# Four sequence mixers with their FFNs on one core: later head scaling, casts and roots on other engines, and another scheduling mode for the order

## The chip, the cores and the metric

The kernel runs on one core of a Trainium2 chip. TensorE (PE in the profile) multiplies matrices, VectorE (DVE), ScalarE (ACT) and GpSimd (POOL) work on tiles, and SyncE (SP) issues the transfers. Each engine works through its own instruction queue in order, and semaphores tie the queues together. The metric is the device time of one execution in microseconds: 1273.06 us for the kernel before (median of three runs, 1273.02 to 1274.07).

## The reference

Input is one sequence of 256 tokens with 1024 channels in float32. Four layers follow one another, with the mixers HGRN, mLSTM, S5 and HGRN again. After each mixer and after each FFN comes a residual with layer norm:

```python
x = _layernorm(ALPHA * x + h, ln_g[i, 0], ln_b[i, 0])
x = _layernorm(ALPHA * x + _swiglu(x, w_gate_up, w_down), ln_g[i, 1], ln_b[i, 1])
```

The HGRN mixer projects x to queries, forget gates, values and output gates, 8 heads of 128 channels. Its recurrence is computed in parallel form: scores of queries and keys with decay products, times the values. What comes out of a head is scaled by the root of its mean square, multiplied by the output gate, and projected:

```python
o = _head_rmsnorm(_from_chunks(oc), norm_w)          # o * rsqrt(mean(o*o) + eps) * w
o = o.reshape(bsz, seq, D_MODEL) * jax.nn.silu(g)
return o @ w_out
```

mLSTM is a matrix memory with exponential gates, S5 a complex diagonal scan of 64 groups with 64 states, and the FFN is SwiGLU with 2816 hidden channels.

## The kernel before

Every float32 operand of a large product is split in a high and a low part, and each product is three matmuls (`mm3`, L155 to L157; the wide form is L185 and L188). Weights come in units of 1 MB on SyncE's queue. Of each half unit ScalarE casts the high part (L127) and VectorE subtracts it to get the low part (L128); I call an L128 on weights a split. Activations lie transposed in `xx`, high and low, ready as matmul operands. A layer norm (`norm`, L205 to L240) takes token half h: residual and statistics (L221 to L223), the root of the variance (`rsqrt`: a multiply and add L197 and a power L198, both on GpSimd), subtract and scale (L235, L236), a transpose on TensorE (L240), and the split into `xx` (L259 on ScalarE, L260 on VectorE). The last norm has no transpose; it scales in two pieces per half (L228, L230) and each piece is sent to the output.

The HGRN mixer (`hgrn`) works on score groups of two head pairs, (0, 1) and (2, 3). For each, `hgrn_scores` first makes the scores within 32 tokens (L606, L607), then runs levels m = 1, 2, 4, 8, 16, 32, 64: ScalarE copies keys (L616), TensorE makes a small product (L620, and L629 for m = 32 and 64), VectorE puts it in place (L623) and multiplies queries and keys with the decay products of the next level (L592). L652 then makes the scores across the halves. Between the levels the program text puts pieces of the projections for values (`v1`) and output gates (`g0`, `g1`), 144 matmuls in all; they are independent of the scores. `heads_out(n)` makes the outputs of four heads (L505, L507), their squares (L509) and sums (L510), the root on GpSimd, and the scaling (L515); `turn` multiplies by the gate (L519) and transposes (L413).

The S5 mixer runs eight blocks: TensorE makes a block's inputs (L1115), VectorE turns them, scans them and turns them back (L1158 to L1169, state in `s5hs`), TensorE makes the outputs of two blocks (L1127) and transposes them (L1133), and L1138 writes the low part of the transposed outputs, for which the output projection waits.

The program text does not fix the order of instructions. `tile.TileContext` schedules the whole program when it is built: it chooses the order within each engine's queue from the dependencies, the program's order, priorities and its own estimate of when things are ready. What stands in a queue then stays in that order on the chip.

The last FFN block (`dproj` with `j == last and i == 3`, L338) orders its matmuls by output columns, then by token halves. At the start, `warm_up` issues matmuls on zeros (L74) and `begin` splits the first pieces of x and of the first weights with `halve`, as their transfers land.

Of the kernel before, what the change touches and what calls it, by code (L numbers as in the profile page):

```python
# [17 lines left out]
P = 128  # L18
# [16 lines left out]
class Trunk:  # L35
    def __init__(self, ctx, tc, aps):
        self.ctx, self.tc, self.nc, self.a = ctx, tc, tc.nc, aps
        mk = lambda name, bufs, **kw: ctx.enter_context(tc.tile_pool(name=name, bufs=bufs, **kw))
        self.const = mk("const", 1)
        self.stage = mk("stage", 3)  # L40
        self.split = mk("split", 8)
        self.xp = mk("xp", 3)
        self.gbp = mk("gbp", 1)
        self.small = mk("small", 4)
        self.ps = mk("ps", 2, space=bass.MemoryType.PSUM)
        self.dram = mk("dram", 1, space=bass.MemoryType.DRAM)
        self.n = 0
        c = self.const
        self.ident = c.tile([P, P], F32, name="ident")
        self.root = c.tile([P, 8], F32, name="root")  # L50
        self.nc.gpsimd.memset(self.root, -0.5)
        self.xx = c.tile([P, KD, 2, S], F32R, name="xx")
# [14 lines left out]
    def warm_up(self, pool):  # L67


        z = pool.tile([P, 512], BF16, name="warm")  # L70
        self.nc.vector.memset(z, 0.0)
        ps = self.bank("t")
        for _ in range(7):
            self.nc.tensor.matmul(ps, z[:, 0:P], z, start=True, stop=True)  # L74


# [53 lines left out]
    def begin(self, pool):  # L130

        src = pool.tile([P, KD, S + 512], F32, name="first")
        out = [self.pair() for _ in range(4)]
        for k, n in ((0, 1), (1, 1), (2, 1), (3, 1), (4, 2), (6, 2)):
            self.nc.sync.dma_start(src[:, k : k + n], self.a["first"][:, k : k + n])
            self.halve(src[:, k : k + n, 0:S], self.xh[:, k : k + n], self.xl[:, k : k + n])
            wide = lambda y: (y if n == 2 else y[:, k % 2 * 512 : (k % 2 + 1) * 512]).rearrange("p (k c) -> p k c", k=n)
            self.halve(src[:, k : k + n, S:], *(wide(y) for y in out[k // 2]))
        for i in range(2):
            self.ready[self.plan[i]] = out[2 * i : 2 * i + 2]  # L140
        self.staged = 2
        self.nc.sync.dma_start(self.ident, self.a["c_ident"])
# [50 lines left out]
    def rsqrt(self, v, n, eps, mul=1.0):  # L193

        t = self.small.tile([P, 2, 8], F32, tag="rs", name=self.uid("rs"))
        w, q = t[:, 0, :n], t[:, 1, :n]
        self.nc.gpsimd.tensor_scalar(w, v, mul, eps, ALU.mult, ALU.add)  # L197
        self.nc.gpsimd.tensor_tensor(q, w, self.root[:, 0:n], ALU.pow)  # L198
        return q

# [13 lines left out]
    def norm(self, h, banks, gb, last=None, perm=False, rev=False):  # L214
# [6 lines left out]
            nc.vector.scalar_tensor_tensor(z[:, c], self.x[h][:, c], ALPHA, banks[n], ALU.mult, ALU.add)  # L221
            nc.vector.bn_stats(st[:, n, :], z[:, c])
        nc.vector.bn_aggr(mv, st)  # L223
        r = self.rsqrt(mv[:, 1:2], 1, LN_EPS)
        if last is not None:
            cuts = slice(0, 512), slice(512, D)
            for c in cuts:
                nc.vector.scalar_tensor_tensor(z[:, c], z[:, c], mv[:, 0:1], gb[:, 0, c], ALU.subtract, ALU.mult)  # L228
            for c in cuts:
                nc.vector.scalar_tensor_tensor(z[:, c], z[:, c], r, gb[:, 1, c], ALU.mult, ALU.add)  # L230
                nc.sync.dma_start(last[h * P : (h + 1) * P, c], z[:, c])
            return
# [213 lines left out]
    def hgrn(self, j, gb, lb=None):  # L446
# [3 lines left out]
        with tc.tile_pool(name=self.uid("hg"), bufs=1, reuse_waits="tile") as hp, \  # L450
# [44 lines left out]
            def heads_out(n):  # L495
# [13 lines left out]
                    nc.scalar.activation(s, po[h], AF.Square)  # L509
                    nc.vector.tensor_reduce(ss[:, h], s.rearrange("p (a b) -> p a b", a=4), AX.X, ALU.add)  # L510
                r = self.rsqrt(ss.rearrange("p a b -> p (a b)"), 8, HEAD_EPS, 1.0 / P)
                for h in range(2):
                    on[n, h] = wp.tile([P, 512], F32, tag="q", name=self.uid("on"), bufs=4)
                    f4 = lambda x: x.rearrange("p (a b) -> p a b", a=4)
                    nc.vector.tensor_tensor(f4(on[n, h]), f4(po[h]), r[:, 4 * h : 4 * h + 4, None].broadcast_to([P, 4, P]), ALU.mult)  # L515

            def turn(n, h):
                o, gate = on[n, h], g[:, h, n * 512 : (n + 1) * 512]
# [35 lines left out]
            scores((2, 3), ([lambda: heads_out(0)], g0[0:1], g0[1:2], g0[2:3], g0[3:], g1[0:1], g1[1:2], g1[2:3]))  # L554
            gb = gb()
            g1[3]()
            for h in range(2):
                turn(0, h)
            heads_out(1)
            self.out_proj(("w_ho", j), gb, ot, lambda h: turn(1, h))  # L560

    def hgrn_gates(self, wp, pr, pf, lb):
# [812 lines left out]
```

## Time and profile before

| | |
|---|---|
| median of three runs | 1273.06 us (1273.02 to 1274.07) |
| the profiled execution | 1272.88 us |
| its span, first to last instruction | 1271.1 us |
| TensorE busy | 1252.0 us |
| VectorE busy | 958.8 us |
| ScalarE busy | 711.9 us |
| GpSimd busy | 54.6 us |
| mean granted TensorE clock | 0.999 |

The span is that of one profiled execution. A line of a group gives source line, engine, operation, output and inputs, shape and count, then busy time and mean duration in ns, then the idle time of the engine just before the instructions and what ended it. A line of the timeline gives the start in us and the duration first. Matmuls overlap in the pipeline: a row's duration is longer than the distance to the next row's start, so the pace is read from the starts.

### The profile page before, as it was taken

What the parts mean: (1) busy time and instruction counts of PE and PEld (TensorE: products, weight loads), DVE (VectorE), ACT (ScalarE), POOL (GpSimd) and SP (SyncE); (2) the same over time, 40 slices, a digit from 0 to 9 for tenths busy, and PEclk for the clock granted to TensorE, in tenths of its full rate; (3) what the DMA queues carried; (4) which work ended last, traced back from release to release, by engine and by line L of the source; (5) the groups of instructions that cost most, each with busy time, mean ns of one, the idle gap of its engine ahead of it and who ended that gap; (6) DMA issues with size and microseconds to landing.
All of it is one profiled execution on the core that took longest, in us unless ns stands there. A gap on an engine that the chain in (4) does not pass through costs nothing.

```text
span 1271.1 us, 20366 instructions
## 1 busy us (share of the span) xinstructions
PE 1252.0 (98%) x7939; PEld 1047.4 (82%) x7939; DVE 958.8 (75%) x1716; ACT 711.9 (56%) x1158; POOL 54.6 (4%) x78
## 2 busy tenths in 40 slices
PE   9999999999999999999999999999999999999997
PEld 7977788888798888888878778888879778888885
DVE  6877889876787799866599797666595887766664
ACT  6755576675467555666443355555459654555550
POOL 0000200000200110000000000000010001000001
PEclk9999999999999999999999999999999999999999
DMA  8733465765373276756477647555554432755530
GB/s 312 293 134 134 159 223 207 274 243 199 113 277 134 100 259 224 246 207 244 163 273 277 244 166 247 184 199 183 182 189 185 165 121 106 271 173 192 193 139 33
DMA packets 46463, 249.93 MB, mean 197 GB/s; under 512 B 5632, under 2 KB 10128, under 8 KB 20000
## 3 DMA queue, kind: packets, MB, share of 16 engines
q1 hardware_dynamic: 46240, 248.55, 54.4%
q8 instruction: 62, 1.02, 0.3%
q14 instruction: 33, 0.27, 0.1%
q0 software_dynamic: 128, 0.09, 0.0%
HBM read 234.99 MB, written 13.63 MB: 196 GB/s over the span
## 4 chain that ended last, share of the span: by engine, by line
PE 92%; DVE 3%; ACT 2%; issue 1%; POOL 1%; DMA 0%; POOLq 0%; DVEq 0%; ACTq 0%
PE g L185 19%; PE g L155 10%; PE g L157 10%; PE g L156 10%; PE g L188 10%; PE a L155 9%; PE a L156 9%; PE a L157 8%; PE t L240 1%; PE t L1127 1%; PE g L1115 1%; DVE lo L128 1%; PE a L620 1%; PE t L1024 1%; PE a L505 0%
## 5 line engine op out<-in xcount | busy, mean ns | idle before, releaser
L128 DVE TENSOR_TENSOR lo<-w,hi 128x1024 fp32r<-128x1024 f32 x389 | 472.7, 1222 | 115.3 <-ACT hi L127 108.3
L127 ACT CAST hi<-w 128x1024 fp32r<-128x1024 f32 x389 | 406.6, 1051 | 189.0 <-PE a L156 109.1
L185 PE MATMUL g<-xx,hi 128*128 128x512 f32 x1024 | 358.3, 395 | 0.0
L188 PE MATMUL g<-xx,lo 128*128 128x256 f32 x1024 | 267.5, 281 | 0.0
L185 PEld LDWEIGHTS g<-xx,hi 128*128 128x128 f32 x1024 | 186.9, 188 | 34.3
L188 PEld LDWEIGHTS g<-xx,lo 128*128 128x128 f32 x1024 | 192.4, 188 | 10.4
L155 PE MATMUL g<-hi,xx 128*128 128x512 f32 x416 | 169.3, 408 | 4.0 <-ACT xx L259 2.9
L156 PE MATMUL g<-hi,xx 128*128 128x512 f32 x416 | 166.6, 401 | 0.0
L157 PE MATMUL g<-lo,xx 128*128 128x512 f32 x416 | 166.4, 403 | 0.0
L156 PE MATMUL a<-hi,hl 128*128 128x512 f32 x344 | 135.8, 395 | 0.0
L155 PE MATMUL a<-hi,hh 128*128 128x512 f32 x344 | 135.5, 396 | 0.0
L157 PE MATMUL a<-lo,hh 128*128 128x512 f32 x344 | 135.4, 394 | 0.0
L319 ACT COPY sum<-g 128x256 f32<-128x256 f32 x128 | 47.6, 372 | 141.3 <-PE g L185 141.0
L320 DVE TENSOR_TENSOR sum<-g,sum 128x256 f32<-128x256 f32 x128 | 54.3, 424 | 67.2 <-ACT sum L319 66.7
L155 PEld LDWEIGHTS g<-hi,xx 128*128 128x128 f32 x416 | 78.8, 190 | 22.9 <-ACT xx L259 4.7
L157 PEld LDWEIGHTS g<-lo,xx 128*128 128x128 f32 x416 | 78.7, 189 | 17.9 <-DVE lo L128 0.7
L156 PEld LDWEIGHTS g<-hi,xx 128*128 128x128 f32 x416 | 78.9, 190 | 16.0 <-issue 0.2
L156 PEld LDWEIGHTS a<-hi,hl 128*128 128x128 f32 x344 | 64.8, 188 | 14.9 <-DVE hl L309 0.3
L157 PEld LDWEIGHTS a<-lo,hh 128*128 128x128 f32 x344 | 64.7, 188 | 14.8
L155 PEld LDWEIGHTS a<-hi,hh 128*128 128x128 f32 x344 | 64.3, 188 | 13.7 <-ACT hh L308 0.6
L156 PE MATMUL g<-xx,lo 128*128 128x256 f32 x200 | 56.6, 283 | 0.0
L157 PE MATMUL g<-xx,hi 128*128 128x256 f32 x200 | 56.5, 283 | 0.0
(303 smaller groups left out, 1779.4 us busy)
## 6 DMA issues: line engine op xcount, KB each, us to landing
w<-in_w_gu SPq DMA_DIRECT2D x88, 1024.0 KB, 4.9
w<-in_w_dn SPq DMA_DIRECT2D x44, 1024.0 KB, 4.9
w<-in_w_hg SPq DMA_DIRECT2D x30, 1024.0 KB, 5.1
w<-in_w_ml SPq DMA_DIRECT2D x12, 1024.0 KB, 4.9
gb<-in_ln SPq DMA_DIRECT2D x8, 1024.0 KB, 4.7
w<-in_w_ho SPq DMA_DIRECT2D x8, 1024.0 KB, 4.9
w<-in_w_so SPq DMA_DIRECT2D x8, 1024.0 KB, 6.2
ct<-s5ct SPq DMA_DIRECT2D x8, 768.0 KB, 7.8
```

Of the source, the lines that this page charges most:

```text
L127: self.nc.scalar.copy(hi, x)
L128: self.nc.vector.tensor_tensor(lo, x, hi.bitcast(F32), ALU.subtract)
L155: mm(ps, lh, rh, start=start, stop=False)
L156: mm(ps, ll, rh, start=False, stop=False)
L157: mm(ps, lh, rl, start=False, stop=stop)
L185: whole = lambda: mm(ps, hi[:, c], self.xx[:, k].rearrange("p i t -> p (i t)"), start=k == 0, stop=k == KD - 1)
L188: mm(ps[:, S:], lo[:, c], self.xh[:, k], start=False, stop=False)
L240: nc.tensor.transpose(pt[:, (k % 4) * P : (k % 4 + 1) * P], z[:, k * P : (k + 1) * P], self.ident)
L319: nc.scalar.copy(t, ps[:, S:])
L320: nc.vector.tensor_tensor(t, ps[:, 0:S], t, ALU.add)
L620: nc.tensor.matmul(pl[rows(c)].rearrange("p (h a t) -> p a h t", h=2, a=2)[:, i], kk[:, i * P + 32 * c : i * P + 32 * c + 32], view(q, i * ...
L1024: nc.tensor.transpose(ps[:, x * P : (x + 1) * P], k["bz"][:, i, 4 * e + x].rearrange("p j g c -> p (j g c)"), self.ident)
```

## The change

- A tile of one column holds the norms' epsilon.
- Nine warm-up matmuls are issued instead of seven.
- In `begin`, the high part of x is cast by VectorE for the first two pieces and by ScalarE for the rest.
- In `rsqrt`, the multiply and add of a single column (all layer norms) runs on VectorE; the power stays on GpSimd.
- In the last norm, the second token half takes its root on ScalarE (Sqrt, with a table load) and a reciprocal on VectorE, and scales piece by piece.
- `heads_out` returns its scaling as a function; for the first four heads of an HGRN layer it is called after the third step of the second score group.
- `TileContext` gets `schedule_with_timeline_sim=True`: the scheduler takes its estimate of time from another machine model, and the order of all engines' queues is made anew.

```diff
@@ warm_up
-        for _ in range(7):
+        for _ in range(9):
@@ begin
-            self.halve(src[:, k : k + n, 0:S], self.xh[:, k : k + n], self.xl[:, k : k + n])
+            x = src[:, k : k + n, 0:S]
+            (self.nc.vector.tensor_copy if k < 2 else self.nc.scalar.copy)(self.xh[:, k : k + n], x)
+            self.nc.vector.tensor_tensor(self.xl[:, k : k + n], x, self.xh[:, k : k + n].bitcast(F32), ALU.subtract)
@@ rsqrt
-        self.nc.gpsimd.tensor_scalar(w, v, mul, eps, ALU.mult, ALU.add)
+        (self.nc.vector if n == 1 else self.nc.gpsimd).tensor_scalar(w, v, mul, eps, ALU.mult, ALU.add)
         self.nc.gpsimd.tensor_tensor(q, w, self.root[:, 0:n], ALU.pow)
@@ norm
-        r = self.rsqrt(mv[:, 1:2], 1, LN_EPS)
+        if last is not None and h:
+            sd, r = (self.small.tile([P, 1], F32, tag=t, name=t, bufs=1) for t in ("sd", "rl"))
+            self.table("sqrt_and_others")
+            self.act(sd, mv[:, 1:2], AF.Sqrt, bias=self.eps)
+        else:
+            r = self.rsqrt(mv[:, 1:2], 1, LN_EPS)
         if last is not None:
-            cuts = slice(0, 512), slice(512, D)
-            for c in cuts:
+            for n in range(2):
+                c = slice(n * 512, (n + 1) * 512)
                 nc.vector.scalar_tensor_tensor(z[:, c], z[:, c], mv[:, 0:1], gb[:, 0, c], ALU.subtract, ALU.mult)
-            for c in cuts:
+                if h and n == 0:
+                    nc.vector.reciprocal(r, sd)
                 nc.vector.scalar_tensor_tensor(z[:, c], z[:, c], r, gb[:, 1, c], ALU.mult, ALU.add)
@@ hgrn, heads_out
                 r = self.rsqrt(ss.rearrange("p a b -> p (a b)"), 8, HEAD_EPS, 1.0 / P)
-                for h in range(2):
-                    ...
+                def scaled():
+                    for h in range(2):
+                        ...
+                return scaled
@@ hgrn
-            scores((2, 3), ([lambda: heads_out(0)], g0[0:1], g0[1:2], ...
+            late = []
+            scores((2, 3), ([lambda: late.append(heads_out(0))], g0[0:1], g0[1:2] + [lambda: late.pop()()], ...
-            heads_out(1)
+            heads_out(1)()
@@ kernel
-    with tile.TileContext(nc) as tc:
+    with tile.TileContext(nc, schedule_with_timeline_sim=True) as tc:
```

The lines of the changed kernel lie a few numbers later: L155 to L157 become L159 to L161, L620 becomes L635, L629 L644, L413 L423, L128 L130, L221 and L222 L225 and L226, L228 and L230 L237 and L240, L1138 L1153, L1158 to L1169 L1173 to L1184.

The order moves on all engines. Three places follow. The first is TensorE's queue in the first HGRN layer, in the levels m = 2 to 16 of the second score group. Before, matmuls of the gate projection (into the banks `g`) stand between the levels' products (into `a`):

```order
L620 MATMUL a155_1180<-q97_779,kk156_1181 32x2x16 x8
L620 MATMUL a157_1195<-q112_900,kk158_1196 32x2x16 x8
L157 MATMUL g159_1210<-lo132_1041,xx_81 128x512
...
L155 MATMUL g160_1211<-hi131_1040,xx_81 128x512
L620 MATMUL a166_1234<-q97_779,kk167_1235 32x2x16 x8
L156 MATMUL g160_1211<-hi131_1040,xx_81 128x512
...
L156 MATMUL g159_1210<-hi162_1214,xx_81 128x512
L620 MATMUL a168_1249<-q112_900,kk169_1250 32x2x16 x8
```

In the changed kernel the same stretch up to the product of level 32 is:

```order
L635 MATMUL a153_1180<-q97_783,kk154_1181 32x2x16 x8
L635 MATMUL a155_1195<-q112_904,kk156_1196 32x2x16 x8
L635 MATMUL a164_1234<-q97_783,kk165_1235 32x2x16 x8
L635 MATMUL a166_1249<-q112_904,kk167_1250 32x2x16 x8
L635 MATMUL a170_1280<-q97_783,kk171_1281 32x2x16 x8
L635 MATMUL a172_1295<-q112_904,kk173_1296 32x2x16 x8
L635 MATMUL a179_1332<-q97_783,kk180_1333 32x2x16 x8
L635 MATMUL a181_1347<-q112_904,kk182_1348 32x2x16 x8
L423 MATMUL t204_1531<-ident_78,on168_1276 128x128 x4
L423 MATMUL t205_1539<-ident_78,on169_1278 128x128 x4
L644 MATMUL a183_1376<-q97_783,k51_418 32x32 x8
```

All projection matmuls have moved ahead: between the first L606 and the first L629 of the second group stood 48 of them, now none; up to the last L413 of the layer stood 72 more, now 48. The 144 pieces of values and gates all stand in the first score group.

The second place is VectorE's queue in the S5 mixer, around the first L1138 (L1153), which writes the low part of the transposed outputs into `xx`. Before:

```order
L1168 TENSOR_TENSOR s5hs2_6931<-t1290_7216,t1291_7217 128x4x64
L1169 TENSOR_TENSOR s5hs2_6931<-t1290_7216,t1291_7217 128x4x64
L1138 TENSOR_TENSOR xx_81<-t1286_7200,xx_81 128x4x2x64
L1158 TENSOR_TENSOR t1296_7238<-g1285_7191,cs1272_7102 128x512
L1159 TENSOR_TENSOR t1297_7239<-g1285_7191,cs1272_7102 128x512
L128 TENSOR_TENSOR lo1311_7271<-w1307_7264,hi1310_7270 128x1024
```

and with the change:

```order
L1180 TENSOR_TENSOR t1326_7370<-g1325_7363,cs1283_7188 128x512
L1181 TENSOR_TENSOR t1327_7371<-g1325_7363,cs1283_7188 128x512
L1173 TENSOR_TENSOR t1332_7392<-g1321_7345,cs1294_7228 128x512
L1153 TENSOR_TENSOR xx_83<-t1286_7204,xx_83 128x4x2x64
L1174 TENSOR_TENSOR t1333_7393<-g1321_7345,cs1294_7228 128x512
```

It stood after the third block's states and now stands within the sixth block's first products, behind five blocks. On TensorE, 40 instead of 24 matmuls of the input projection's second half stand ahead of the first L1115, and of the splits between the first L1158 and the last L1138, 12 became 8 on VectorE.

The third place is the end of VectorE's queue, the last norm of both token halves. Before, `x2272` (first half) is done before `x2276` (second half) begins, but two transposed hidden tiles' parts (L296, L309) stand between, and TensorE's last matmuls of the first half came earlier:

```order
L228 SCALAR_TENSOR_TENSOR x2272_12715<-x2272_12715,mv2274_12717,gb2022_11381 128x512 x2
L230 SCALAR_TENSOR_TENSOR x2272_12715<-x2272_12715,rs2275_12723,gb2022_11381 128x512 x2
L296 TENSOR_TENSOR hd2268_12681<-sg2267_12680,g2266_12655 128x256
L309 TENSOR_TENSOR hl2271_12694<-t2269_12690,hh2270_12693 128x256
L221 SCALAR_TENSOR_TENSOR x2276_12732<-x1967_11128,a1977_11175 128x512
L222 BN_STATS st2277_12733<-x2276_12732 128x6
```

With the change:

```order
L319 TENSOR_TENSOR hl2271_12698<-t2269_12694,hh2270_12697 128x256
L227 BN_AGGR mv2274_12721<-st2273_12720 128x2
L201 TENSOR_SCALAR rs2275_12727<-mv2274_12721 128x1
L237 SCALAR_TENSOR_TENSOR x2272_12719<-x2272_12719,mv2274_12721,gb2022_11385 128x512 x2
L240 SCALAR_TENSOR_TENSOR x2272_12719<-x2272_12719,rs2275_12727,gb2022_11385 128x512 x2
L225 SCALAR_TENSOR_TENSOR x2276_12736<-x1967_11132,a1977_11179 128x512
L225 SCALAR_TENSOR_TENSOR x2276_12736<-x1967_11132,a1978_11180 128x512
L226 BN_STATS st2277_12737<-x2276_12736 128x6 x2
```

The first half's passes moved behind the last hidden tile's L309 (L319). On TensorE the twelve last matmuls of the first half (L338, now L348) stood far ahead of the end; now they stand three matmuls and two transposes ahead of the second half's twelve, which now alternate between both output columns.

More of the change, by code (lines that the diff above doesn't have):

```diff
@@ L51, in __init__ @@
         self.nc.gpsimd.memset(self.root, -0.5)
+        self.eps = c.tile([P, 1], F32, name="eps")
+        self.nc.gpsimd.memset(self.eps, LN_EPS)
         self.xx = c.tile([P, KD, 2, S], F32R, name="xx")
@@ L511, in heads_out @@
                 r = self.rsqrt(ss.rearrange("p a b -> p (a b)"), 8, HEAD_EPS, 1.0 / P)
-                for h in range(2):
-                    on[n, h] = wp.tile([P, 512], F32, tag="q", name=self.uid("on"), bufs=4)
-                    f4 = lambda x: x.rearrange("p (a b) -> p a b", a=4)
-                    nc.vector.tensor_tensor(f4(on[n, h]), f4(po[h]), r[:, 4 * h : 4 * h + 4, None].broadcast_to([P, 4, P]), ALU.mult)
+                def scaled():
+                    for h in range(2):
+                        on[n, h] = wp.tile([P, 512], F32, tag="q", name=self.uid("on"), bufs=4)
+                        f4 = lambda x: x.rearrange("p (a b) -> p a b", a=4)
+                        nc.vector.tensor_tensor(f4(on[n, h]), f4(po[h]), r[:, 4 * h : 4 * h + 4, None].broadcast_to([P, 4, P]), ALU.mult)
+                return scaled
             def turn(n, h):
@@ L553, in hgrn @@
             scores((0, 1), ([], [lambda: query(2)], [], [lambda: query(3)], v1[0:1], v1[1:2], v1[2:3], v1[3:]))
-            scores((2, 3), ([lambda: heads_out(0)], g0[0:1], g0[1:2], g0[2:3], g0[3:], g1[0:1], g1[1:2], g1[2:3]))
+            late = []
+            scores((2, 3), ([lambda: late.append(heads_out(0))], g0[0:1], g0[1:2] + [lambda: late.pop()()], g0[2:3], g0[3:], g1[0:1], g1[1:2], g1[2:3]))
             gb = gb()
```

## The prediction

> **What bounds the kernel now.** I read the first page of the profile first, for who is busy and what the chain that ended last is made of:
>
> ```profile
> span 1271.1 us, 20366 instructions
> PE 1252.0 (98%) x7939; PEld 1047.4 (82%) x7939; DVE 958.8 (75%) x1716; ACT 711.9 (56%) x1158; POOL 54.6 (4%) x78
> PE 92%; DVE 3%; ACT 2%; issue 1%; POOL 1%; DMA 0%; POOLq 0%; DVEq 0%; ACTq 0%
> ```
>
> TensorE is busy for 1252.0 of 1271.1 us and is 92% of the chain. Its work does not change, so the time can fall by a few us only; it can rise by as much as the new order leaves TensorE without work. The waits of TensorE say what there is to win, and the windows where another engine is nearly as full as TensorE say what there is to lose:
>
> ```profile
> PE g L155 <- ACT xx L259: 2.9, 5, 0.7
> PE a L620 <- DVE near L623: 2.3, 2, 1.2
> PE t L1127 <- DVE s5hs L1168: 1.3, 1, 1.3
> ...
> 82.00:104.00 22.00, 20.82 (x335) 15.11 (x334) 17.64 (x57) 10.66 (x19) 2.08 (x2) 1.00 0.25 93
> 104.00:126.00 22.00, 22.00 (x147) 18.21 (x145) 17.00 (x29) 11.14 (x25) 1.85 (x2) 1.00 0.53 192
> 682.00:725.00 43.00, 41.10 (x299) 32.79 (x298) 39.62 (x64) 14.97 (x19) 0.00 (x0) 1.00 0.74 277
> ```
>
> (In the windows the columns after the length are TensorE, its weight loads, VectorE, ScalarE, GpSimd, granted clock, DMA share.) The largest waits come to 6.5 us. In 82 to 104 us, the second score group of the first HGRN layer, and in 682 to 725 us, the S5 scan, VectorE is busy 80% and 92%: there a VectorE chain runs, and TensorE is full only because projection matmuls stand between the chain's own. I call those fillers. Their price is the pace of TensorE, from two rows that stand ten matmuls apart, (109.63 − 107.32)/10 = 0.231 us:
>
> ```profile
> 107.32 0.39 PE L156 MATMUL g<-hi,xx 128*128 128x512 f32 x1
> ...
> 109.63 0.40 PE L157 MATMUL g<-lo,xx 128*128 128x512 f32 x1
> ```
>
> **The change part by part.** The new scheduling mode moves nearly every instruction, so the edits are priced in the order that results. First the **second score group** of an HGRN layer (heads 4 to 7). Its marks now, with the costs of its VectorE work between the first two:
>
> ```profile
> 82.77 0.38 PE L606 MATMUL a<-q,k 128*32 128x32 f32 x21
> 103.01 0.46 PE L629 MATMUL a<-q,k 128*32 128x32 f32 x32
> 106.39 0.65 PE L629 MATMUL a<-q,k 128*32 128x64 f32 x32
> 109.87 1.06 PE L652 MATMUL a<-q,k 128*128 128x128 f32 x8
> 125.49 0.52 PE L413 MATMUL t<-ident,on 128*128 128x128 f32 x3
> ...
> L592 DVE TENSOR_TENSOR q<-q,f 128x256 f32<-128x256 f32 x8 | 3.4, 420 | 0.0
> L592 DVE TENSOR_TENSOR k<-k,f 128x256 f32<-128x256 f32 x8 | 3.4, 420 | 0.0
> L623 DVE COPY_PREDICATED near<-msk,a 128x64 f32<-128x64 int32 x10 | 2.5, 255 | 0.9 <-PE a L620 0.7
> L128 DVE TENSOR_TENSOR lo<-w,hi 128x1024 fp32r<-128x1024 f32 x2 | 2.4, 1218 | 0.0
> L515 DVE TENSOR_TENSOR on<-a,rs 128x512 f32<-128x512 f32 x2 | 1.3, 686 | 1.8 <-POOL rs L198 1.8
> ```
>
> From 82.77 to 103.01 are 20.24 us, in which 48 fillers stand: 48 × 0.231 = 11.1, so 9.1 us is not filler. After the change all value and gate fillers stand in the first score group, and these levels have none between them. There the time is VectorE's: 17.64 × 20.24/22 = 16.2 us busy now, less the two weight splits (2.4), plus two gate products moved in (1.4), plus the 0.9 of waits on TensorE's small results: 16.1. So the uncovered time grows from 9.1 to 16.1: **+7.0** (+6.1 with no wait left; +9.4 if each of the eight small-matmul groups costs 0.3 more). The 1.8 that VectorE loses to GpSimd's root before L515 is spared by the later head scaling, and is in this: the multiply no longer holds the levels behind it in the queue. Without that edit +7.0 would be +8.8.
>
> From 103.01 to 125.49 are 22.48 us with 72 fillers (16.6), so 5.9 not filler. After: 48 fillers (11.1), in four places. 21 of them (4.9) cover the 3.4 us to the second L629; 3 (0.7) do not cover the 3.5 us to L652, which lose a split and a product: 2.8 left. Then L652, its copies and the head outputs, 3.8, and 24 fillers (5.5) over square, sum, GpSimd's root (1.9, below), scaling, gate: 6.2. With 0.5 for L629 that is 18.9, less 11.1 is 7.8: **+1.9** (0 to +4). The first score group, with fewer and longer runs of fillers, gives **−0.9** back, an estimate out of the 2.3 that TensorE waits before L620 in all (0 to −2.3). First layer +8.0. In the last HGRN layer two more splits stand between the levels (2.3): **+10.3**. Both: +18.3, bounds +10 to +27.
>
> **S5.** The scan is eight blocks of one VectorE chain:
>
> ```profile
> 659.51 2.67 PE L1115 MATMUL g<-s5u,bm 128*128 128x64 f32 x23
> 661.44 0.69 DVE L1158 TENSOR_TENSOR t<-g,cs 128x512 f32<-128x512 f32 x1 [2.46 <-PE g L1115]
> ...
> L128 DVE TENSOR_TENSOR lo<-w,hi 128x1024 fp32r<-128x1024 f32 x12 | 14.6, 1223 | 0.0
> L1163 DVE TENSOR_TENSOR_SCAN g<-s5rr,t 128x256 f32<-128x256 f32 x16 | 10.2, 680 | 0.0
> L1138 DVE TENSOR_TENSOR xx<-t,xx 128x512 fp32r<-128x512 f32 x4 | 4.4, 1092 | 5.0 <-ACT xx L89 5.0
> ```
>
> After, 40 instead of 24 fillers stand before the first L1115 (16 × 0.231 = 3.7 us later), and the first L1138, which releases the output-projection fillers, stands behind five blocks instead of three, so TensorE has nothing but the scan's small matmuls for about two blocks. Against this, four of the twelve splits (4.9) leave the chain, and L1138 no longer waits. Up to the fourth output turn 11 fewer fillers are done (2.5 us), and the chain arrives some 0.3 later by these rows: +2.8. I take **+4**, since two later blocks also wait for the fillers that L1138 holds; bounds 0 (the chain shortens by all 4.9) to +8 (the late start counts whole).
>
> **Norms and stage changes.** The epsilon moves from GpSimd to VectorE in 15 norms:
>
> ```profile
> 134.68 1.21 DVE L128 TENSOR_TENSOR lo<-w,hi 128x1024 fp32r<-128x1024 f32 x1
> 134.86 1.07 POOL L197 TENSOR_SCALAR rs<-mv 128x1 f32<-128x1 f32 x1 [7.05 <-DVE mv L223]
> 135.81 0.87 DVE L235 SCALAR_TENSOR_TENSOR x<-x,mv,gb 128x256 f32<-128x256 f32 x2
> 136.02 0.70 POOL L198 TENSOR_TENSOR rs<-rs,root 128x1 f32<-128x1 f32 x1
> 92.72 1.65 POOL L198 TENSOR_TENSOR rs<-rs,root 128x8 f32<-128x8 f32 x1
> ```
>
> The 1.07 hop lies under a split and two L235, and TensorE's waits for xx are 2.9 in all: that is the most this can win. But after, four L235 stand ahead of the first L236 (0.9 more), then a split (1.2) and the other half's L221. At eight stage changes this is up to 8 × 1.0; I take it as bare at four, less half of the 2.9: **+2.5** net, bounds −3 to +8. **FFN and mLSTM**: the S5 preparation now stands in unbroken runs on VectorE between the sums of the first two FFNs, and six mLSTM heads come without fillers. VectorE is 75% busy and splits made earlier cover most of it; I count one split's length (1.22) late in each of two FFNs: **+2.5**, bounds 0 to +6.
>
> **Head.** Two casts move to an idle VectorE, and two warm-ups are added:
>
> ```profile
> 5.24 0.80 PE L155 MATMUL g<-hi,xx 128*128 128x512 f32 x1 [0.89 <-ACT hi L127]
> 10.30 0.62 ACT L127 CAST xx<-first 128x512 fp32r<-128x512 f32 x1 [0.92 <-DMA first<-in_first]
> ```
>
> The first matmul can come 0.4 earlier, but the fifth piece waits for its transfer at 10.30 anyway; two warm-ups (0.85) fit the gap of 0.89. **−0.3**, bounds −1.5 to 0.
>
> **Tail.**
>
> ```profile
> 1262.50 0.62 PE L338 MATMUL a<-hi,hl 128*128 128x512 f32 x2
> 1263.88 0.69 DVE L222 BATCH_NORM_STATS2 st<-x 128x6 f32<-128x512 f32 x1
> 1264.86 1.42 DVE L228 SCALAR_TENSOR_TENSOR x<-x,mv,gb 128x512 f32<-128x512 f32 x2
> 1265.74 0.93 POOL L198 TENSOR_TENSOR rs<-rs,root 128x1 f32<-128x1 f32 x1
> 1266.71 1.41 DVE L230 SCALAR_TENSOR_TENSOR x<-x,rs,gb 128x512 f32<-128x512 f32 x2 [0.44 <-POOL rs L198]
> ```
>
> The root on ScalarE spares the 0.44 and costs a reciprocal of about 0.1; the table load lies on an idle ScalarE. But with E for the last matmul's end, the first token half's L228 and L230 (2.83) now stand before the second half's two L221 and two L222 (2.76). The first half's sums are ready at E − 3.7, so its passes end at E + 1.4; then 2.76, 0.2, and 2.98 for the last passes: E + 7.3, where L230 now ends at E + 5.0. **+2.3**, bounds +1 to +3.5.
>
> Sum: 18.3 + 4 + 2.5 + 2.5 − 0.3 + 2.3 = +29.3. The span becomes 1300.4; the profiled execution, 1272.88, lies 1.78 outside its span and 0.18 below the median 1273.06, so about 1302.
>
> **The rivals.** *The new order is neutral and the edits count* (faster). One mechanism: shorter hops to roots. If the score levels stay covered, the change wins two waits before L515 (2 × 1.8), at most 2.9 at the norms, 0.4 in the tail and 0.3 in the head: 1273.1 − 7.2 = 1266. For it speaks that TensorE's own work is unchanged; against it, that VectorE's 16 us of level work has no filler beside it in the new order. It decides if that chain is under 9 us.
>
> *Only the HGRN stages and the tail pay*: 18.3 + 2.3 − 0.3 gives 1293; S5's shorter chain, and norms without the GpSimd hop, speak for it.
>
> *The clock falls too.* TensorE's pace was half at the start and the granted clock half after the end:
>
> ```profile
> 7.96 0.63 PE L155 MATMUL g<-hi,xx 128*128 128x512 f32 x1
> 8.68 0.39 PE L155 MATMUL g<-hi,xx 128*128 128x512 f32 x1
> 1268.00:1269.00 1.00, 0.00 (x0) 0.00 (x0) 0.12 (x1) 0.00 (x0) 0.00 (x0) 0.51 0.65 250
> ```
>
> It rose between those two matmuls, 7 us after the first warm-up, and fell 4.9 us after the last matmul. If sixteen us of small matmuls count as idle, each bare stretch is followed by up to 7 us at half pace, a loss of 3.5; two per HGRN layer make 14: 1316. Against it: in 82 to 104 us the clock stayed 1.00, though with fillers there. The Trainium skill, "TensorE: Matmul & The Clock Gate" (section "What's actually happening"), says that the gate goes to half after an idle window of about 3.4 us and comes back after a busy one; no run here shows yet what a stretch of small matmuls counts as.
>
> *The order stays as it was*, and the edits alone give about 1267: the order of the changed kernel excludes it nearly.
>
> **How the numbers follow.** Forecast 0.55 (1302, own range 1291 to 1313); HGRN and tail only 0.18 (1293); clock too 0.15 (1316); shorter hops with a neutral order 0.07 (1266); between these, no change, 0.03; order as before 0.02. A measurement of this kernel tells 0.2%, or 2.5 us, from no change: slower 0.88, same 0.03, faster 0.09. The bounds of the terms reach from +9 to +54, but not all at once: range 1282 to 1322.
>
> **What would show it.** In the profile after, TensorE should fall to about a third busy for 16 us in each second score group, waiting for L623's and L592's successors, with VectorE full. It should wait at the S5 scan for the first output turn. The last pass should end 7 us after the last matmul. I am wrong if TensorE stays 98% busy, or if it loses time outside these places; a clock under 1.00 behind the score groups is the third rival.

## The result and the profile after

The changed kernel takes **1376.17 us** (1373.03 to 1377.03), the kernel before 1273.04: 1.0804 times as long, 95% interval 1.0785 to 1.0822. The forecast was 1302, range 1282 to 1322. The sign was right and the size was under a third of it: 103 us lost, where 29 were forecast.

The first page of the changed kernel's profile (busy times, then the chain that ended last, by engine):

```profile
span 1375.0 us, 20411 instructions
PE 1286.2 (94%) x7941; PEld 1076.6 (78%) x7941; DVE 965.0 (70%) x1734; ACT 706.5 (51%) x1155; POOL 40.8 (3%) x62
PE 84%; DVE 10%; ACT 2%; issue 2%; DMA 1%; POOL 0%; SPq 0%; DVEq 0%; ACTq 0%
```

VectorE has 10% of the chain instead of 3%. TensorE's busy time has grown by 34 us with two matmuls more, so some of its work ran more slowly or overlapped less. Its idle time within the span has grown from 19 to 89 us: that is two thirds of the loss. The waits of TensorE in the changed kernel (what waited, for what; us in all, times, longest):

```profile
PE t L250 <- DVE xx L270: 20.0, 6, 4.6
PE t L250 <- DVE x L246: 17.5, 9, 6.5
PE t L423 <- DVE on L533: 9.4, 4, 4.0
PE a L635 <- DVE q L607: 8.4, 6, 1.9
PE a L635 <- DVE near L638: 4.1, 3, 1.9
PE g L159 <- ACT oh L269: 2.7, 1, 2.7
```

L250 is the transpose of a norm (L240 before), L245 and L246 are its subtract and scale (L235 and L236), L269 and L270 the split into `xx` (L259 and L260). L250 waits for 37.5 us at the stage ends; before, L240 waited for nothing, and the norms' only wait was the 2.9 for `xx`. Of the 37.5, 20.0 are waits for a split L270, which frees the bank `t` that the next transposes write. L635 is a score level, L423 the transpose of the scaled heads.

To see which stage lost how much, I took the start of the sixteenth transpose of each norm (L240, now L250) from the timelines of both kernels, and subtracted. The growth of that difference from norm to norm is the loss of the stage between:

| stage up to the end of its norm | lost, us |
|---|---|
| first HGRN | 24.6 |
| FFN | 12.0 |
| mLSTM | 9.6 |
| FFN | 8.0 |
| S5 | 14.8 |
| FFN | 7.1 |
| last HGRN | 27.7 |
| last FFN and the tail | 0.1 |

What one stage end looks like shows best at the end of the first FFN. Ahead of the two rows of TensorE stands VectorE's first residual of the first token half; before:

```profile
326.39 1.39 DVE L221 SCALAR_TENSOR_TENSOR x<-x,a 128x512 f32<-128x512 f32 x2 [1.10 <-PE a L157]
...
333.66 0.39 PE L157 MATMUL a<-lo,hh 128*128 128x512 f32 x1
334.00 0.38 PE L240 MATMUL t<-ident,x 128*128 128x128 f32 x2
...
339.39 0.38 PE L240 MATMUL t<-ident,x 128*128 128x128 f32 x2
```

and after:

```profile
359.07 0.68 DVE L225 SCALAR_TENSOR_TENSOR x<-x,a 128x512 f32<-128x512 f32 x1
...
363.01 0.39 PE L161 MATMUL a<-lo,hh 128*128 128x512 f32 x1
366.39 0.41 PE L250 MATMUL t<-ident,x 128*128 128x128 f32 x2 [2.99 <-DVE x L246]
367.26 0.72 PE L159 MATMUL g<-hi,xx 128*128 128x512 f32 x2 [0.46 <-ACT xx L269]
368.14 0.41 PE L250 MATMUL t<-ident,x 128*128 128x128 f32 x2 [0.15 <-DVE x L246]
371.10 0.69 PE L250 MATMUL t<-ident,x 128*128 128x128 f32 x2 [2.55 <-DVE xx L270]
371.44 0.78 PE L160 MATMUL g<-hi,xx 128*128 128x512 f32 x1
372.01 0.63 PE L161 MATMUL g<-lo,xx 128*128 128x512 f32 x1
372.44 0.63 PE L159 MATMUL g<-hi,xx 128*128 128x512 f32 x1
...
375.59 0.38 PE L250 MATMUL t<-ident,x 128*128 128x128 f32 x2
```

From residual to first transpose it is 7.6 us before and 7.3 after: up to there the norm has not become longer. But before, TensorE multiplied all through it, with the second half's last products: 48 matmuls of 512 columns start between the residual and the half's eighth transpose (the last row of each fence). After, most of these had been issued earlier, the last one starts at 363.01, 23 remain in all, and TensorE stands still. The row with the eighth transpose comes 16.5 us after the residual instead of 13.0. The other two FFN ends look alike, with 18 matmuls instead of 46 and 48.

At the ends of the HGRN and mLSTM stages it is another thing. There 44 matmuls stand between residual and eighth transpose before and 44 to 46 after, so the cover is still there, but the eighth transpose comes 18.4 to 19.4 us after the residual instead of 11.3 or 11.4. The end of the first HGRN layer, before:

```profile
138.34 0.42 DVE L260 TENSOR_TENSOR xx<-t,xx 128x256 fp32r<-128x256 f32 x1
138.67 0.88 DVE L236 SCALAR_TENSOR_TENSOR x<-x,rs,gb 128x256 f32<-128x256 f32 x2
```

and after:

```profile
161.93 0.48 DVE L246 SCALAR_TENSOR_TENSOR x<-x,rs,gb 128x256 f32<-128x256 f32 x1
...
163.47 0.68 DVE L225 SCALAR_TENSOR_TENSOR x<-x,a 128x512 f32<-128x512 f32 x1
...
164.68 1.21 DVE L130 TENSOR_TENSOR lo<-w,hi 128x1024 fp32r<-128x1024 f32 x1
165.80 0.42 DVE L270 TENSOR_TENSOR xx<-t,xx 128x256 fp32r<-128x256 f32 x1
166.27 0.69 PE L250 MATMUL t<-ident,x 128*128 128x128 f32 x2 [4.14 <-DVE xx L270]
```

Before, the first split into `xx` stood ahead of the last two scalings. Now it stands behind all four, behind weight splits (L130) and behind the second half's residual (L225), and TensorE waits 4.14 us for it. Up to the eighth transpose TensorE is idle for 5.1 to 5.7 us at these three ends, where it was idle for 0.1 or 0.2.

At all these ends the clock falls as well: behind the waits of the first FFN's end the matmuls start 0.43 us apart instead of 0.23. The windows of the changed kernel (length, then TensorE, weight loads, VectorE, ScalarE, GpSimd busy, granted clock, DMA) show it there, and in the second score group of the first HGRN layer:

```profile
366.00:371.00 5.00, 1.54 (x6) 0.70 (x6) 5.00 (x14) 0.74 (x2) 1.24 (x2) 0.74 0.15 25
371.00:375.00 4.00, 3.90 (x11) 3.13 (x11) 3.96 (x13) 0.37 (x1) 0.67 (x1) 0.50 0.56 233
103.60:122.50 18.90, 10.62 (x257) 9.29 (x256) 16.56 (x53) 6.01 (x15) 2.02 (x2) 0.73 0.17 62
```

Counting the matmuls of 512 columns whose next neighbour starts 0.41 to 0.445 us later gives 75, against 16 before. At 0.195 us more each, the 59 cost 11.5 us; this leaves out all smaller matmuls, so it is a lower bound of the clock's part. How much of the other 22.7 us of longer busy time is the clock's was not separated.

### The profile page after: what moved, and what is told of

It reads as the page before. It is cut to its first block, busy times and chain, and to the rows that moved or that the text cites. A ratio compares the mean times of both kernels' runs of the same rounds, so it can differ in the third digit from the quotient of the medians.

```text
span 1375.0 us, 20411 instructions
## 1 busy us (share of the span) xinstructions
PE 1286.2 (94%) x7941; PEld 1076.6 (78%) x7941; DVE 965.0 (70%) x1734; ACT 706.5 (51%) x1155; POOL 40.8 (3%) x62
## 4 chain that ended last, share of the span: by engine, by line
PE 84%; DVE 10%; ACT 2%; issue 2%; DMA 1%; POOL 0%; SPq 0%; DVEq 0%; ACTq 0%
PE g L189 17%; PE g L159 9%; PE g L160 9%; PE g L161 9%; PE g L192 9%; PE a L159 7%; PE a L160 7%; PE a L161 7%; DVE lo L130 3%; PE g L1130 1%; DVE x L225 1%; DVE st L226 1%; PE t L1142 1%; PE t L250 1%; DVE x L245 1%
## 5 line engine op out<-in xcount | busy, mean ns | idle before, releaser
L130 DVE TENSOR_TENSOR lo<-w,hi 128x1024 fp32r<-128x1024 f32 x389 | 470.3, 1222 | 129.3 <-ACT hi L129 122.5
L189 PE MATMUL g<-xx,hi 128*128 128x512 f32 x1024 | 362.5, 395 | 0.0
L192 PE MATMUL g<-xx,lo 128*128 128x256 f32 x1024 | 267.1, 281 | 0.0
L159 PE MATMUL g<-hi,xx 128*128 128x512 f32 x416 | 169.4, 416 | 2.5 <-ACT xx L269 2.3
L160 PE MATMUL g<-hi,xx 128*128 128x512 f32 x416 | 170.8, 412 | 0.0
L161 PE MATMUL g<-lo,xx 128*128 128x512 f32 x416 | 167.0, 406 | 0.1
L161 PE MATMUL a<-lo,hh 128*128 128x512 f32 x344 | 135.3, 394 | 0.0
L159 PE MATMUL a<-hi,hh 128*128 128x512 f32 x344 | 131.6, 397 | 1.4 <-ACT hh L318 1.4
L159 PEld LDWEIGHTS g<-hi,xx 128*128 128x128 f32 x416 | 80.0, 195 | 22.0 <-ACT xx L269 3.5
L161 PEld LDWEIGHTS g<-lo,xx 128*128 128x128 f32 x416 | 81.5, 196 | 18.6 <-DVE lo L130 0.5
L160 PEld LDWEIGHTS g<-hi,xx 128*128 128x128 f32 x416 | 82.1, 197 | 16.7
L160 PEld LDWEIGHTS a<-hi,hl 128*128 128x128 f32 x344 | 64.6, 188 | 17.5 <-DVE hl L319 3.5
L161 PEld LDWEIGHTS a<-lo,hh 128*128 128x128 f32 x344 | 64.6, 188 | 14.7
L159 PEld LDWEIGHTS a<-hi,hh 128*128 128x128 f32 x344 | 64.1, 188 | 14.6 <-ACT hh L318 2.1
L269 ACT CAST xx<-t 128x256 fp32r<-128x256 f32 x56 | 20.5, 373 | 88.9 <-PE t L250 84.1
L250 PE MATMUL t<-ident,x 128*128 128x128 f32 x112 | 25.0, 315 | 37.7 <-DVE xx L270 20.0
```

The costliest lines, as they stand in the source:

```text
L130: self.nc.vector.tensor_tensor(lo, x, hi.bitcast(F32), ALU.subtract)
L159: mm(ps, lh, rh, start=start, stop=False)
L160: mm(ps, ll, rh, start=False, stop=False)
L161: mm(ps, lh, rl, start=False, stop=stop)
L189: whole = lambda: mm(ps, hi[:, c], self.xx[:, k].rearrange("p i t -> p (i t)"), start=k == 0, stop=k == KD - 1)
L192: mm(ps[:, S:], lo[:, c], self.xh[:, k], start=False, stop=False)
```

## The experiments

**The edits without the mode, and the mode without the edits.** The first is the changed kernel with this one line undone, the second the kernel before with this line alone:

```diff
-    with tile.TileContext(nc, schedule_with_timeline_sim=True) as tc:
+    with tile.TileContext(nc) as tc:
```

> All edits of the change, but the scheduler's mode as before. If the order that the mode makes carries the whole loss, this is near the kernel before: 1266 to 1273 us. The rival is that the edits themselves carry part of it (the epsilon standing in VectorE's queue ahead of the norm's passes, the last norm): then it is above 1290 us.

Measured: 1267.63 us, ratio 0.9949 (0.9937 to 0.9962).

> The kernel before with nothing but the scheduler's other mode. If the mode carries the loss: 1365 to 1390 us, with the waits of TensorE for the norm's VectorE passes (some 37 us after the change). If the edits carry part of it: under 1350 us.

Measured: 1377.38 us, ratio 1.0812 (1.0798 to 1.0827). So the mode carries the whole loss, and the edits gain about 6 us under the old one (5.4 against the 1273.04 above, 6.2 against the runs beside it). Where they gain is read from the marks: the first L606 (now L621) comes at 51.8 instead of 52.6 (head), each HGRN layer gains another 1.7 to 1.8 after that, and the time from the last matmul's end to the span's end is 7.5 instead of 8.0.

**The order of VectorE inside a norm.** My first theory was that VectorE's queue was to blame, since four L245, splits and the second half's L225 stand ahead of what TensorE waits for. The norms' passes were chained by order-only dependencies:

```diff
+    def tie(self, i):          # i stands behind the one tied before it
...
-            nc.vector.scalar_tensor_tensor(z[:, c], z[:, c], mv[:, 0:1], gb[:, 0, c], ...)
-            nc.vector.scalar_tensor_tensor(z[:, c], z[:, c], r, gb[:, 1, c], ALU.mult, ALU.add)
+            self.tie(nc.vector.scalar_tensor_tensor(z[:, c], z[:, c], mv[:, 0:1], gb[:, 0, c], ...))
+            self.tie(nc.vector.scalar_tensor_tensor(z[:, c], z[:, c], r, gb[:, 1, c], ALU.mult, ALU.add))
```

and likewise the first half's last split and both residuals of the second half behind it.

> The changed kernel, with VectorE's order inside a norm tied: subtract, scale and split of each piece follow one another, and the second half's residual comes behind the first half's last split. If the order of VectorE's queue in the norms makes TensorE's 37 us of waits for transposes (and the half clock behind them), 1325 to 1345 us. If TensorE has simply used up the matmuls that covered the norms, the tie changes little: 1365 us or more.

Measured: 1394.33 us, 18 slower than the changed kernel. TensorE's waits there:

```profile
PE t L261 <- DVE x L257: 17.8, 11, 3.1
PE t L261 <- DVE xx L283: 9.8, 9, 2.2
PE t L436 <- DVE on L546: 8.9, 4, 4.0
PE g L159 <- ACT xx L282: 8.3, 14, 1.0
```

The waits for the split of `xx` halve, but the second half's norm now begins later, and TensorE waits more elsewhere (8.3 us for ScalarE's part of `xx`, where it was 2.3). The edit ties the passes, the first half's last split and the second half's residuals; the other splits into `xx` and the weight splits stay where the mode puts them, so this is not VectorE's order from before. That this tie alone mends the norms is refuted; what VectorE's old order does is tested below.

**Covering matmuls put back by hand.** Four kernels tie TensorE's order, again by order alone. First the pieces behind a level of the second score group, then those of both groups (the diff shows this form), then the second token half's products at stage ends, then the last two together:

```diff
@@ scores
                     for f in todo:
-                        f()
+                        with tc.issue_after(self.mark.ins):   # the level's last matmul
+                            f()
@@ ffn (and likewise part(1, 0), part(1, 1) in out_proj)
+            with self.behind():                               # behind the first half's last matmul
-            up((1,), last)
-            dproj((1,), last - 1, lambda: turn((1,), last))
-            dproj((1,), last)
+                up((1,), last)
+                dproj((1,), last - 1, lambda: turn((1,), last))
+                dproj((1,), last)
```

> The changed kernel, with the projection pieces that the program text puts behind a level of the second score group tied behind that level's product on TensorE, as they stood before. By the forecast's first term the second score group loses 9 us in the first and 10 in the last HGRN layer, and more with the half clock behind it: 1350 to 1358 us. If the levels were not bare for the lack of fillers but wait for VectorE all the same, 1370 us or more.

Measured: 1373.14 us. This is in the range of the rival. The second group is covered again and the first went bare (windows of this run, columns as above; TensorE is idle for 8.5 of the first 25 us, and what the next expectation calls 14 us lost is not to be read from this row):

```profile
75.00:100.00 25.00, 16.55 (x327) 14.92 (x326) 16.91 (x50) 10.07 (x27) 0.00 (x0) 0.74 0.25 86
100.00:125.00 25.00, 25.00 (x291) 20.04 (x291) 21.17 (x60) 12.65 (x29) 2.02 (x2) 0.92 0.17 61
```

In the changed kernel these rows stand the other way round:

```profile
75.00:100.00 25.00, 25.00 (x288) 21.91 (x288) 18.32 (x42) 14.25 (x28) 0.00 (x0) 1.00 0.47 169
100.00:125.00 25.00, 16.36 (x340) 13.38 (x339) 21.00 (x67) 10.82 (x30) 2.02 (x2) 0.75 0.25 86
```

> The changed kernel, with the projection pieces behind a level tied to that level's product in both score groups (the run before tied the second group only, and the first went bare instead: TensorE lost 14 us there between 75 and 100 us). If bare levels are what the HGRN layers lose before their norm, both layers get back 10 to 12 us: 1352 to 1357 us. If the pieces' place does not matter in the whole, 1370 us or more.

Measured: 1370.20 us, 6 less than the changed kernel instead of 20 or more, just inside the rival's range. By the marks the two HGRN layers get back 6.6 and 4.0 us, and S5 loses 1.6 more.

> The changed kernel, with TensorE's order tied at the ends of the HGRN, mLSTM and FFN stages: the second token half's last products stand behind the first half's last product, as the program text has them, so that they run while VectorE normalises the first half. If these covering matmuls, used up early, are what the norms lost, six of seven stage ends get back 5 to 8 us each: 1328 to 1345 us. If VectorE's passes are late for another reason, 1365 us or more.

Measured: 1366.41 us, 10 less instead of 31 to 48, in the rival's range. By the marks, the first two FFNs and mLSTM give back 3 to 5 us each, the third FFN and the HGRN layers nothing. So the used up cover is a part of the loss at FFN ends and not the whole, and the rival, late passes of VectorE, stands beside it.

> Both ties at once. If the two losses are separate and both are a matter of used up cover, the gains add: 1305 to 1325 us. If one cover is taken from the other, less than the better of the two plus 10 us.

Measured: 1357.88 us, 18 less: the gains add, but leave 85 of the 103 us, and the time lies in the range of the second case and not in that of the first. All four gave less than expected, so cover put back in these places by hand is not enough. That the queue around it is still made for another time is my reading; these runs do not show it.

**Whole queues exchanged.** So I took the order that each engine's queue has under the old mode and imposed it on the new one: the list of an engine's instructions is written into the kernel, and each gets an order-only dependency on its predecessor. The mode then orders the remaining engines around it.

```diff
+def tie_order(tc, nc):
+    by = {i.name: i for i in nc.cur_bb.bb.instructions}
+    ...
+        for p, i in zip(row, row[1:]):
+            tc.add_manual_dep(i, p.name, dep, reason="engine order")
...
         trunk(tc, aps, out)
+        tie_order(tc, nc)
```

> The changed kernel under the new mode, with TensorE's queue tied to the order that it has under the old mode; the mode orders the other engines around it (402 of VectorE's 1734 instructions stand elsewhere than in the changed kernel, 446 elsewhere than under the old mode). If the loss is TensorE's order (matmuls that should cover are used up early), 1268 to 1300 us. If it is VectorE's order, which stays the mode's, 1340 us or more.

Measured: 1334.52 us, between the two ranges: TensorE's order is a part of the loss.

> The same with VectorE's queue tied to its old order, and TensorE's left to the mode. If the loss is VectorE's order (weight splits and other work ahead of the pass that TensorE waits for), 1270 to 1310 us. If it is TensorE's, 1340 us or more.

Measured: 1389.41 us. VectorE's old order does mend the HGRN and mLSTM ends: from residual to eighth transpose TensorE is idle there for 0.5 us each, where the changed kernel has 5.1 to 5.7. At the FFN ends 6.8 to 7.2 us remain (6.3 to 7.2), with 27 to 29 covering matmuls instead of 46 to 48. Where the run loses again what it wins was not traced.

> Both queues tied to their old order, ScalarE, GpSimd and SyncE left to the mode. If the two queues are all there is to the loss, 1266 to 1275 us, as the edits alone without the mode (1267.6). If ScalarE's order or the order of transfers bears part of it, 1285 us or more.

Measured: 1293.70 us. The two queues are most of the loss, and not all of it.

> The other way round: the edits under the old mode, with TensorE's queue tied to the order that the new mode gave it. If TensorE's order is the loss, 1340 to 1380 us. If VectorE's order is, under 1300 us, since here the old mode orders VectorE around it.

Measured: 1380.61 us. TensorE's order from the new mode loses as much as the change itself, though the old mode orders everything else. But it orders it around TensorE: by the starts in the trace, at least 388 of VectorE's 1734 instructions and 195 of ScalarE's stand elsewhere than in the edits under the old mode (463 and 230 in the changed kernel). So the run shows what follows from TensorE's order, and not what that order costs with VectorE's as it was. The cleaner comparison is the repairs: TensorE's order alone gives back 42 us; VectorE's alone gives nothing (13 slower); both together give back 82. By stage (differences to before at the marks, as in the table above):

| stage | changed | TensorE's order old | TensorE's and VectorE's old | edits, old mode |
|---|---|---|---|---|
| first HGRN | 24.6 | 7.5 | 5.5 | −2.6 |
| FFN | 12.0 | 9.4 | 2.8 | 0.1 |
| mLSTM | 9.6 | 9.3 | 0.2 | −0.6 |
| FFN | 8.0 | 9.0 | 2.8 | 1.3 |
| S5 | 14.8 | 14.5 | 11.5 | 0.2 |
| FFN | 7.1 | 3.0 | −0.8 | −0.8 |
| last HGRN | 27.7 | 6.8 | 0.1 | −1.7 |
| last FFN, tail | 0.1 | −1.2 | −1.3 | −1.2 |

In the HGRN layers TensorE's order is most of it. At most other stage ends TensorE's order alone changes little, and it needs VectorE's as well. TensorE's waits in the run with its own old order alone:

```profile
PE t L250 <- DVE x L246: 19.1, 9, 4.0
PE t L313 <- DVE hd L306: 9.0, 5, 2.7
PE g L1130 <- DMA bm<-s5b: 5.2, 2, 4.9
```

and with VectorE's old order too:

```profile
PE g L1130 <- DMA bm<-s5b: 7.2, 1, 7.2
PE g L159 <- DVE k L586: 5.7, 2, 5.5
PE g L159 <- ACT xx L269: 3.0, 5, 0.8
```

The norms wait as under the old mode. Left are above all one wait for a transfer in S5 and one for the gates of the first layer. Two more kernels each add one queue, ScalarE's or SyncE's, to the two that were tied:

> As the run with TensorE's and VectorE's queues tied to the old order (1293.7 us), with ScalarE's queue tied too; transfers and GpSimd are left to the mode. TensorE waits there 7.2 us for the transfer of bm in S5 and 5.5 for the gates in the first layer. If ScalarE's order is behind both, 1268 to 1274 us. If the order of transfers is behind the S5 wait, 1278 to 1288 us.

Measured: 1283.57 us; the wait for the gates is down to 2.5, and the transfer's remains:

```profile
PE g L1130 <- DMA bm<-s5b: 7.0, 1, 7.0
PE g L159 <- ACT xx L269: 3.2, 5, 0.9
PE g L159 <- ACT f L91: 2.5, 1, 2.5
```

> The same with SyncE's queue of transfers tied instead of ScalarE's. If the transfers' order is behind the S5 wait, 1279 to 1286 us, with the wait for bm gone and the 5.5 for the gates left. If it is ScalarE's, 1290 us or more.

Measured: 1282.28 us, the wait for bm gone; the wait for the gates, expected to stay, went as well (5.7 to 0.3). ScalarE's order gives back 10.1, SyncE's 11.4. If they added, 1272.2 would result, 4.5 above the edits under the old mode; a kernel with both was not run. By the marks ScalarE's order gives its part back in the first HGRN layer (3.4), the first two FFNs (2.4 and 1.5) and the last HGRN layer (1.7), SyncE's in S5 (6.8) and the first HGRN layer (4.7). In S5 some 4 us come back with neither, and their cause is open.

**Single edits.** The later head scaling, alone in the kernel before:

```diff
-            scores((2, 3), ([lambda: heads_out(0)], g0[0:1], g0[1:2], ...
+            scores((2, 3), ([lambda: late.append(heads_out(0))], g0[0:1], g0[1:2] + [lambda: late.pop()()], ...
```

> The kernel before with the later head scaling alone. If VectorE's 1.8 us wait for GpSimd's root before the scaling stood on the path in both HGRN layers, 3.2 to 3.6 us less than before: 1269.5 to 1270.5 us. If the levels had room, no change: 1272.5 to 1273.5 us.

Measured: 1269.93 us, ratio 0.997 (0.996 to 0.998), by the medians the larger part of what the edits gain; by the marks 1.6 and 1.4 us in the two layers. In the run with all edits, VectorE's wait before the scaling of the first four heads is zero (first HGRN layer):

```profile
L527 DVE TENSOR_TENSOR on<-a,rs 128x512 f32<-128x512 f32 x2 | 1.3, 686 | 0.0
```

And the edits under the old mode with the epsilon back on GpSimd:

```diff
-        (self.nc.vector if n == 1 else self.nc.gpsimd).tensor_scalar(w, v, mul, eps, ALU.mult, ALU.add)
+        self.nc.gpsimd.tensor_scalar(w, v, mul, eps, ALU.mult, ALU.add)
```

> The edits under the old mode, but the norms' epsilon back on GpSimd. If the hop of 1.07 us lies under other work at the stage ends, the same as with it on VectorE, 1267 to 1269 us. If it stood on the path in several norms, 1270 to 1273 us.

Measured: 1269.55 us, ratio 0.9967 (0.9955 to 0.998), beside 0.9949 (0.9937 to 0.9962) with it on VectorE. The intervals overlap, so a gain of up to 2 us by the epsilon is neither shown nor excluded. In the two profiled runs 0.9 of the difference lies ahead of the first score, where no norm stands (the first L621 at 52.65 and 51.77).

## Why the prediction was right or wrong

**The edits' gain** (rival: 7.2 us in a neutral order) was right in kind: about 6, of which by the medians the two head scalings are the larger part, as the 1.8 us wait had said. What was wrong is that a neutral order could come with the mode.

**First term, second score group, 9.1 to 16.1 us uncovered.** The mechanism is there: no projection matmul stands in the levels. But they took 18.9, not 16.1:

```profile
103.62 0.27 PE L621 MATMUL a<-q,k 128*32 128x32 f32 x8
122.55 0.28 PE L644 MATMUL a<-q,k 128*32 128x32 f32 x4
146.12 0.44 PE L423 MATMUL t<-ident,on 128*128 128x128 f32 x2 [3.98 <-DVE on L533]
```

**Second stretch, 18.9 us forecast,** took 146.12 − 122.55 = 23.6: with a fallen clock in its first fillers, and 4.0 of wait for the scaled heads where I had 0.7. The first layer lost 20.6 us up to that row; 24 more output products were done by then (24 × 0.231 = 5.5), so 15.1 against my 8.0. The last layer comes to some 18 in the same way, against 10.3. That the cost would be cured by fillers between the levels, as this term implied, is not borne out: moved back, they gave 6.6 and 4.0 us in the two layers. The first score group needed them as much.

**S5, +4:** 14.8 with its norm. The count of fillers was wrong: by the traces 9 matmuls of the projection's second half stand ahead of the first L1115 before and 40 after, not 24 and 40, and from the norm's mark to that product it is 7.9 us longer, not 3.7. The time from there to the last output turn is 64.6 us instead of 64.5, with 27 fewer matmuls of 512 columns in it, so the four splits that left the chain did not make it shorter. The other 6.8 us come behind the last turn, where TensorE waits 6.5 for the norm's L246. The wait for the transfer of bm is 1.7 here; it is 7.2, of 11.5 lost, only where TensorE's and VectorE's queues are repaired, and SyncE's queue I had not read.

**Norms and stage changes, +2.5 (−3 to +8), and FFN and mLSTM, +2.5 (0 to +6).** This is the step that failed. I asked what stands ahead of L236 on VectorE, priced the delay at 1.0 per stage, and took it as bare at four of eight. Two things were wrong. First, I did not ask what TensorE would do meanwhile: I had counted fillers in the score groups only, though the second token half's products do the same at each norm, and at the three FFN ends 18 to 23 of them are left of 46 to 48. Second, the delay is not ahead of the first scaling, which moves by 0.7 to 1.4 us at the HGRN, mLSTM and FFN ends, near the price I gave, but behind it: the splits into `xx` stand so late on VectorE that at the HGRN and mLSTM ends the eighth transpose comes 7.1 to 8.1 us later after the residual than before. In the seven norms with transposes TensorE is idle for 43 us between the first residual and the sixteenth transpose; before, it was 3. The FFN and mLSTM stages lost 36.7 us together, and the HGRN layers some 9 each at their norms, behind the row at 146.12 and its like. Together that is some 55 us against the 5.0 of these two terms. The prediction had named such a sign: it is wrong if TensorE loses time outside the listed places.

**Tail, +2.3:** the last passes moved behind as foretold, but less:

```profile
1364.97 1.07 PE L348 MATMUL a<-hi,hl 128*128 128x512 f32 x4
1366.30 1.28 DVE L225 SCALAR_TENSOR_TENSOR x<-x,a 128x512 f32<-128x512 f32 x2
1370.58 1.42 DVE L240 SCALAR_TENSOR_TENSOR x<-x,rl,gb 128x512 f32<-128x512 f32 x2
```

The last matmul ends at 1366.05 and the last pass at 1372.0, E + 6.0 instead of my E + 7.3: the first half's passes were done at E + 0.3, a microsecond earlier than worked out. The last FFN and the tail together lost 0.1, so +2.3 did not come.

**The clock** was a rival at 0.15, and it fell in nearly every stage that went bare. What a return costs differs. At the first FFN's end the half pace lasts from 371.44 to 375.00, 3.6 us, a loss of some 1.8, not 3.5. The Trainium skill, "TensorE: Matmul & The Clock Gate" (section "What's actually happening"), has about 3.4 us of busy work for the return; by that row the trace agrees. Behind the bare levels of the first HGRN layer it is near the 3.5 that I had:

```profile
123.00:131.00 8.00, 7.63 (x36) 5.55 (x27) 3.59 (x10) 1.85 (x9) 0.00 (x0) 0.59 0.00 0
```

TensorE is busy for nearly all of the 8 us at a mean clock of 0.59, so up to 8 × 0.41 = 3.3 us are lost. In all the clock is at least 11.5 of the 103 us.

**The range** was too narrow since I added the terms of a few places that I had looked at, while the order had changed everywhere. The bounds of the terms as listed add to +6.5 and +52.5, not to +9 and +54; the measured 103 lies far above both.

## What to carry to other kernels

When a change remakes the order of all queues, count for every wait of another engine, not only the longest chain, how much independent TensorE work stands beside it before and after; what is issued earlier there is missing later. Count also what stands on the other engine ahead of the operation that frees TensorE's bank, not only ahead of the one that feeds it. To find which queue carries the loss, pin one engine's whole order at a time: here TensorE's old order gave 42 of 109 us back, VectorE's old order nothing alone and 41 more on top of it. The scheduler moves the other engines around what is pinned, so read in each such run how far they moved. A scheduling mode is a change of its own and is timed by itself: the edits of this change are worth 0.5% under the old mode, and that kernel, at 1267.6 us, is the one to keep.

## What the runs showed of the hardware

The granted clock fell though TensorE was never idle for long: in the 18.9 us of bare score levels TensorE has records for 10.6 us, with no gap above 1.9, and the mean granted clock is 0.73. At the first FFN's end it fell within a stretch of 8 us that held a gap of 3.0, one of 2.6 and six matmuls. In S5 it stayed at half while TensorE had records nearly throughout:

```profile
730.25:743.91 13.66, 12.41 (x72) 11.81 (x72) 13.59 (x28) 0.80 (x2) 0.00 (x0) 0.50 0.61 215
```

These are the scan's matmuls of 64 and 128 columns. In the changed kernel's span the stretches at half pace, but for those at its start and end, last 3.4, 6.8, 10.2 or 13.7 us, each a multiple of 3.4. At the tail of the kernel before it fell 4.9 us after the last matmul. I had expected small matmuls to count as work.
